# The prices of tensor engine instructions in the planner of a two-layer streaming encoder step

## The chip, the core and the metric

The kernel runs as one launch on one core of a Trainium2 chip. The metric is device time in microseconds, from runs of the whole program. The core has a tensor engine (PE in the profile, its weight loads PEld), a vector engine (DVE), a scalar engine (ACT), GpSimd (POOL) and SyncE (SP), which issues most of the transfers. Each engine takes its own instructions strictly in the order in which the program lists them and waits on semaphores for what other engines make.

## The reference, cut to what matters

One inference step of a two-layer encoder for 384 tokens of width 1024: a sample group of 8 streams with 16 tokens each, and a prompt of 256 tokens. The two groups share all weights.

```
for each layer i:
    x += 0.5 * post(SwiGLU_1(pre(x)))        # 1024 -> 2816 -> 1024
    x +=       post(Mixer_i(pre(x)))         # layer 0: convolution module, layer 1: gated DeltaNet
    x +=       post(MemXAttn(pre(x), mem))   # 4 heads, 256 memory tokens per stream
    x += 0.5 * post(SwiGLU_2(pre(x)))
# pre, post: RMSNorm with gains.  The prompt's memory keys and values: mem @ xa_wk, mem @ xa_wv
```

Everything is float32. Beside the two streams of tokens the step returns the prompt's memory keys and values, the last rows of the convolutions and the recurrent states.

## The kernel before, in words

**Tiling.** Tokens lie in three tiles of 128: the sample group, then two of the prompt. Features lie in tiles of 128 as well. The eight sublayers are called f00, conv, x0, f01, f10, dn, x1 and f11 here, for feed-forward, convolution, cross-attention and DeltaNet of layers 0 and 1.

**Products.** A float32 weight chunk of 128 x 1024 is loaded (`raw`), rounded by ACT to a part `whi` and completed by DVE to a part `wlo` (method `get`). The activations are split likewise (`hTh`, `hTl`, or `rbh`, `rbl`). A product is then three matmuls in the type F32R. Projections (`gmm`) have 384 moving columns, one matmul for all tokens; down and output projections (`dmm`) and some first projections (`wide`) have 512. Small products (attention scores, DeltaNet's matrices, the prompt's memory keys and values) are plain float32 matmuls, each of which shows as two records in the profile. The sample group's attention uses `quad`: four products with 32 stationary columns each, which the tensor engine holds side by side; one `quad` shows as eight records. Transposes are matmuls with the identity (`tr`).

**Two stages make the order.** First, class `Emitter` records all operations with a price each, `cost`, in nanoseconds. It carries a running clock of the tensor engine, `vt`, which `mm`, `quad` and `tr` advance by their price. Work beside the main stream (the norms between sublayers in `chain`, attention heads, DeltaNet heads) is written as generators; `pump` and `until` let such a task take its next step once `vt` has reached the time that the task named. So `vt` sets in which order operations are recorded, and with it which PSUM bank and which columns of the shared tile `big` each of them gets.

Second, class `Scheduler` (method `order`) takes the recorded operations with their dependences and makes a list schedule on modelled engines. Each operation has a `path`, the longest way of prices and hand-over times (`LAT`) to the end of the program. Whenever a modelled engine comes free, it takes, of the operations that are ready by then, the one with the largest `path` plus `bonus` (the constants CHB, HALF and RUSH). The order so found is the order of the instructions in every engine's queue, the transfers of SP among them. Dependences between the operations of one PSUM bank are kept by the whole bank, so four `quad`s into one bank are a chain.

**Between sublayers.** `tokenwise` finishes a sublayer token tile by token tile and starts `chain` for each: a square sum on ACT, a root on POOL (`rstd`: an addition and a power), DVE products, a second root, DVE products, eight transposes, and the split. Pieces of the prompt's memory keys and values (`kv`, 32 pieces of 16 float32 matmuls each) depend on little; the main stream offers a number of them at several places, to be used where the tensor engine would stand still. In cross-attention, `head` makes for every head the scores (four `quad`s into one bank, four products of 256 columns into another), softmax, transposes, the products with the values (again four and four), transposes.

Of the kernel before, what the change touches and what calls it, by code (L numbers as in the profile page):

```python
# [17 lines left out]
KT = 8                  # feature tiles of d_model  # L18
NTOK = 384              # columns: 128 of the sample group (8 streams x 16), then 256 of the prompt
TT = 3                  # token tiles: sample, prompt 0, prompt 1  # L20
FF = 22                 # feature tiles of d_ff
NB = 8                  # sample streams
BL = 16                 # tokens of one
NH = 8                  # DeltaNet heads
XH = 4                  # cross-attention heads
MEM = 256
CW = 31
SW = 4
EPS = 1e-6
W = 8                   # split weight chunks on chip  # L30
RAW = 3                 # raw chunks on chip
# order of the first transfers: memory (m), key and value chunks (c), rows (x), identity, gains
START = ["c0a", "m0a", "c0b", "m0b", "m1", "i", "x1", "g", "c1", "x2", "x0", "c2"]
TOLD = CW - BL          # taps that reach no token of the same step
OLD = 10                 # feature tile of the first sublayer from which these are worked on
CHB = 4000.0            # ns by which what belongs to a token tile goes before the same of the next
RUSH = 10000.0          # ns by which a sublayer's last projections go before the rest
NRUSH = 3               # feature tiles that this holds for
SLOTS = 4               # chunks of keys and values on chip at the start
FOUR = ["f01", "f10", "f11", "x0", "x1"]     # sublayers whose first 512 features are made token tile by token tile  # L40
# first projections of a sublayer that begin before the last token tile is there
SPLIT = {"f00": 0, "conv": 0, "x0": 1, "f01": 0, "f10": 0, "dn": 1, "x1": 2, "f11": 0}
# pieces of the memory's keys and values that a place in the program offers the tensor engine
KV = {"start": 3, "f00": 3, "conv": 20, "co": 3, "xo": 0, "f01": 1, "f10": 2, "dn": 6, "f11": 0}
HALF = 1400.0            # ns by which the first half of a row goes before the second
GROUPS = [(0, 1), (2, 3, 4, 5, 6, 7)]   # heads whose decays are made together
TAIL = 3                # down-projection chunks that go token tile by token tile
LANES = 8               # transfers under way on a queue
DMA_IN, DMA_OUT = 650.0, 950.0
HOP = 100.0             # ns from an engine to the next  # L50
BIG = 17300             # words of the shared region

# columns of the per-feature table
# [5 lines left out]
# constant matrices: causal blocks, block sums, decay masks, block-doubling masks  # L59
# [34 lines left out]
class Emitter:  # L94
    """Records the program in issue order. Tasks beside the main stream are advanced by running
    clocks of the engines, so that their matmuls fall where their operands are ready."""
# [141 lines left out]
    def mm(self, out, lhsT, rhs, start, stop, skip=False):  # L238
        n = self._n(rhs)
        if rhs.dtype == F32R:  # L240
            cost = max(107.0, n / 2.4) + 3
        else:
            cost = 2 * max(107.0, n / 1.2) + 2
        self.vt += cost
        t = self.nc.tensor
        kw = {"skip_group_check": True} if skip else {}
        self._add("P", cost, lambda: t.matmul(out, lhsT, rhs, start=start, stop=stop, **kw), [lhsT, rhs], [out])  # L247
        return self.vt + HOP

    def quad(self, mms):  # L250
        """Products into four groups of 32 rows, which the tensor engine works on at once."""
        n = self._n(mms[0][2])
        cost = 2 * max(107.0, n / 1.2) + 85.0
        self.vt += cost
        t = self.nc.tensor

        def go():
            for out, lhsT, rhs, start, stop in mms:
                t.matmul(out, lhsT, rhs, start=start, stop=stop)  # L259
        self._add("P", cost, go, [x for m in mms for x in m[1:3]], [m[0] for m in mms])  # L260
        return self.vt + HOP

# [13 lines left out]
    def get(self, name, dest=None):  # L276
        """The two parts of a weight chunk: loaded and split as early as their room is free."""
        j = self.nchunk
        self.nchunk += 1
        raw = self.raw[j % RAW]  # L280
# [23 lines left out]
class Scheduler:  # L304
    """Orders the recorded program: a list schedule by the longest way to the end, on the engines'
    known costs, that keeps every dependence between the operations."""
# [8 lines left out]
    def cell(self, ap):  # L315
        """(what, bits): the tile and the columns in it that an operand covers."""
# [32 lines left out]
    def graph(self):  # L349
        ops = self.ops  # L350
        readers, writers = {}, {}
        for i, o in enumerate(ops):
# [3 lines left out]
            for what, bits in rs:  # L356
                if what is not None:
                    pred.update(j for b, j in writers.get(what, ()) if b & bits)
                    if what[0:2] == "ps":
                        # two engines don't read a bank at once  # L360
# [79 lines left out]
class Region:  # L440
    """First-fit allocation of the columns of one tile."""
# [5 lines left out]
    def take(self, n, keep=0, high=False):  # L447
# [13 lines left out]
        # of the places at an edge of a hole, the one whose columns were freed the longest ago  # L461
# [19 lines left out]
class Model:  # L481
# [42 lines left out]
    def alloc(self, n, keep=0):  # L524
        """(columns, handle) for the main stream."""
# [19 lines left out]
    def _bank(self):  # L545
# [3 lines left out]
        # the one that has been free for longest  # L549
# [38 lines left out]
    def rows(self, kind, i):  # L588
        """A row of gains on all partitions."""
# [4 lines left out]
    def rstd(self, s1, s2, dep):  # L594
        """(s1 + s2) ** -0.5."""
# [6 lines left out]
    def chain(self, t, y, yb, gpost, gpre, half=False, cross=False):  # L602
        """x += post(y); the next sublayer's normalized input, transposed and split."""
# [8 lines left out]
        if y is not None:  # L612
            ss, s0 = self.st(2), self.st(1)
            f = 4.0 if half else 1.0    # half of the norm: a root of four times the mean square
            for n in range(2):
                # the two banks, one to an engine at a time
# [15 lines left out]
        for n in range(2):  # L632
# [3 lines left out]
            # behind the row stands what its sum of squares is short of  # L636
# [21 lines left out]
    def gmm(self, out, hi, lo, c0=0, c1=NTOK, h=None, l=None):  # L658
        """out[feature, token] of a chunk [k, 8, 128 features] and the transposed activations."""
# [12 lines left out]
    def dmm(self, y, hi, lo, ah, al, first, last, halves=(0, 1)):  # L672
        """y[token, 1024] += activations [k, 128 tokens] times a chunk of rows."""
# [9 lines left out]
    def first_chunks(self, names, chains, split):  # L683
        """The first projections of a sublayer; some of them on two token tiles before the third is there."""
# [18 lines left out]
    def wide(self, o, w, t):  # L703
        """out[token, 512] of a token tile and four pieces of weights [k, 2, 512]."""
# [14 lines left out]
    def turn(self, a, o, e):  # L719
        """Four blocks of columns, transposed."""  # L720
# [11 lines left out]
    def gains(self, post, pre):  # L732
        """Rows of gains: of the norm behind a sublayer and of the next one's."""
# [98 lines left out]
    def tokenwise(self, acc, held, ops, ready, first, gpost, gpre, ghs, before=None, kv=0, late=False, half=False):  # L832
        """The last chunks of a product into the residual, token tile by token tile, each followed by
        its norms in the background."""
# [30 lines left out]
    def kv_open(self, slots=2, order=()):  # L865
        """Room for pieces of the memory's keys and values: the memory, some weight chunks, two results."""
# [14 lines left out]
    def early(self, what, order):  # L881
        """The first transfers of all go in a given order."""
        self.E.bonus = 1e9 - 1e6 * order.index(what) if what in order else 0.0

    def kv_part(self, out, name, what, order):
        """One of the first transfers in two halves, so that the products can begin with the first."""
# [16 lines left out]
    def kv(self, n):  # L903
        """Some pieces of the memory's keys and values. They wait for nothing else and go where the
        tensor engine would stand still."""
# [40 lines left out]
    def old_taps(self):  # L946
        """The taps that reach only tokens of earlier steps for all of a step's tokens."""
# [17 lines left out]
    def conv(self, chains, post, pre):  # L965
# [4 lines left out]
        HW = CW - TOLD + BL - 1     # tokens of a block and those before it that the later taps reach  # L970
# [27 lines left out]
        def taps():  # L998
            for c0 in range(0, KT, 2):
# [5 lines left out]
                for j in range(CW):  # L1005
                    for c in cs:
# [4 lines left out]
                        elif j < TOLD:  # L1011
                            # the prompt's tokens that have a token that far behind
# [236 lines left out]
    def deltanet(self, chains, post, pre):  # L1249
# [40 lines left out]
        def pre_task(o, b, e):  # L1290
            """Gates of all heads and the decays between all tokens."""
# [39 lines left out]
            for hs in GROUPS:  # L1331
# [12 lines left out]
                # one behind the other, so that the scalar engine changes its table once  # L1344
# [5 lines left out]
        def short(o, b, e, ti):  # L1350
            """Short convolution and SiLU of one feature tile; (columns, handle, ready)."""
# [17 lines left out]
        def head(h, q, k, v):  # L1369
# [51 lines left out]
            def unit(t):  # L1421
                """Decayed products of keys and queries, and the inverse's transpose by block doubling."""
# [6 lines left out]
                # blocks of up to 32 tokens lie one below the other in 32 columns: the transposes of the  # L1429
                # inverse so far and of what it makes of the matrix, which one product brings on together  # L1430
# [21 lines left out]
                if t:  # L1452
                    # pairs of blocks of 32 tokens, then the two of 64
# [35 lines left out]
            # sample: the state's part of the keys and queries, even and odd streams apart  # L1489
# [4 lines left out]
            # prompt, first chunk: no state yet  # L1494
# [61 lines left out]
            # output norm and gate  # L1556
# [107 lines left out]
def consts():  # L1664
    """Constant matrices that depend on shapes alone."""
# [13 lines left out]
def pack(inp):  # L1679
    """The inputs in the order in which the program reads them: layout alone."""  # L1680
# [3 lines left out]
    def g_type(a, c0, n=P):  # L1684
        # [1024, n] -> [p, k, n]
# [8 lines left out]
    for n, i in CHUNK.items():  # L1694
# [5 lines left out]
        elif t in ("g4", "u4", "q4"):  # L1700
            # [1024, 512] -> [p, 2 k, 512]
# [29 lines left out]
    # [l, b, m, h, (c p)] -> [l, h, u, p, b, c, m]  # L1731
# [58 lines left out]
```

## Time and profile before

| What | Value |
|---|---|
| Time of three runs | 1892.46, 1894.15, 1896.69 us; median 1894.15 us |
| Span of the profiled execution | 1891.9 us, 27912 instructions |
| Median of the runs less that span | 2.25 us |
| PE busy | 1870.6 us, 99% of the span |
| PEld busy | 1682.6 us, 89% |
| DVE, ACT, POOL busy | 1025.5, 794.5, 168.8 us |
| Mean traffic | 146 GB/s to and from HBM |

The span runs from the first to the last instruction of one profiled execution; the page gives no other time of that execution, and what lies around the span is taken as the 2.25 us to the median. The stages can be told by the rows of the trace: f00 to about 297 us, conv to 515, x0 to 640, f01 and f10 to 1182, dn to 1480, x1 to 1608, f11 to the end. Matmuls overlap, so that a record's mean duration is longer than the time from its start to the next one's start; the latter is what one matmul costs in a row of them.

### The profile page before, as it was taken

How to read it: one execution, taken by the hardware profiler on the slowest of the kernel's cores; microseconds unless marked ns; L12 is line 12 of the kernel's file. 1: busy time of each engine (PE TensorE's matmuls, PEld its weight loads, DVE VectorE, ACT ScalarE, POOL GpSimd, SP SyncE). 2: the span in 40 equal slices, each digit the busy share in tenths (PEclk: the TensorE clock that was granted, in tenths of full speed). 3: DMA queues.
4: the chain of work that ended last, by engine and by line, in shares of the span. 5: the costliest groups of instructions: out<-in, count | busy, mean ns of one | idle time of the engine just before them, and what ended most of it. 6: DMA issues, size and time to landing. Idle time of an engine off the chain costs nothing.

```text
span 1891.9 us, 27912 instructions
## 1 busy us (share of the span) xinstructions
PE 1870.6 (99%) x10863; PEld 1682.6 (89%) x10863; DVE 1025.5 (54%) x1940; ACT 794.5 (42%) x1589; POOL 168.8 (9%) x407
## 2 busy tenths in 40 slices
PE   8999999999999999999999999999999999999998
PEld 7999999999877899999899999989898767899997
DVE  6564436998653633334633344788886734533333
ACT  4333334312643533233433233787786533433332
POOL 1000002111100100000100000323321101000000
PEclk9999999999999999999999999999999999999999
DMA  8544434556685443434533343433324782444431
GB/s 300 179 136 125 134 112 121 128 147 216 219 312 210 156 129 128 134 123 130 163 122 117 120 134 101 128 97 99 123 90 124 236 311 101 134 134 134 122 123 45
DMA packets 88469, 278.83 MB, mean 147 GB/s; under 512 B 18001, under 2 KB 20561, under 8 KB 88337
## 3 DMA queue, kind: packets, MB, share of 16 engines
q1 hardware_dynamic: 86080, 271.42, 44.7%
q0 software_dynamic: 2256, 5.64, 0.9%
q8 instruction: 85, 1.39, 0.3%
q14 instruction: 48, 0.39, 0.1%
HBM read 265.09 MB, written 11.92 MB: 146 GB/s over the span
## 4 chain that ended last, share of the span: by engine, by line
PE 97%; ACT 1%; DMA 1%; DVE 0%; POOL 0%; issue 0%; SPq 0%; DVEq 0%; POOLq 0%; ACTq 0%
PE ps L247 91%; PE ps L266 3%; PE ps L259 2%; DMA raw<-in_w 0%; POOL stat L197 0%; ACT big L190 0%; DMA x<-in_x 0%; DVE big L210 0%; ACT whi L189 0%; SPq L270 0%; ACT big L189 0%; ACT hTl L190 0%; ACT L190 0%; DVE big L197 0%; DVE wlo L197 0%
## 5 line engine op out<-in xcount | busy, mean ns | idle before, releaser
L197 DVE TENSOR_TENSOR wlo<-raw,whi 128x1024 fp32r<-128x1024 f32 x361 | 438.1, 1221 | 570.7 <-ACT whi L189 542.7
L189 ACT CAST whi<-raw 128x1024 fp32r<-128x1024 f32 x361 | 374.5, 1050 | 640.3 <-PE ps L247 584.6
L247 PE MATMUL ps<-hTh,wlo 128*128 128x384 f32 x1680 | 498.3, 341 | 0.0
L247 PE MATMUL ps<-hTl,whi 128*128 128x384 f32 x1680 | 497.1, 342 | 0.0
L247 PE MATMUL ps<-hTh,whi 128*128 128x384 f32 (+1 forms) x1680 | 496.9, 342 | 0.0
L247 PEld LDWEIGHTS ps<-hTl,whi 128*128 128x128 f32 x1680 | 308.9, 188 | 8.0 <-issue 2.1
L247 PEld LDWEIGHTS ps<-hTh,whi 128*128 128x128 f32 x1680 | 308.8, 188 | 7.9 <-issue 1.2
L247 PE MATMUL ps<-big 128*128 128x128 f32 (+5 forms) x1944 | 308.0, 288 | 7.1 <-DMA big<-in_w 6.7
L247 PEld LDWEIGHTS ps<-hTh,wlo 128*128 128x128 f32 x1680 | 308.7, 188 | 6.5 <-issue 2.3
L247 PEld LDWEIGHTS ps<-big 128*128 128x128 f32 (+1 forms) x1944 | 269.6, 190 | 40.3 <-issue 20.8
L247 PE MATMUL ps<-whi,rbh 128*128 128x512 f32 x672 | 206.0, 396 | 0.4 <-ACT big L189 0.4
L247 PE MATMUL ps<-wlo,rbh 128*128 128x512 f32 x672 | 203.8, 395 | 0.0
L247 PE MATMUL ps<-whi,rbl 128*128 128x512 f32 x672 | 202.5, 393 | 0.0
L210 DVE SCALAR_TENSOR_TENSOR big<-big,cols 128x384 f32<-128x384 f32 (+13 forms) x424 | 189.5, 497 | 2.2 <-ACT big L190 0.3
L247 PEld LDWEIGHTS ps<-whi,rbl 128*128 128x128 f32 x672 | 125.7, 188 | 24.7 <-issue 0.4
L247 PEld LDWEIGHTS ps<-wlo,rbh 128*128 128x128 f32 x672 | 125.3, 188 | 24.6 <-issue 0.4
L247 PEld LDWEIGHTS ps<-whi,rbh 128*128 128x128 f32 x672 | 124.8, 188 | 21.1 <-ACT big L189 0.6
L197 DVE TENSOR_TENSOR big<-big,ps 128x64 f32<-128x64 f32 (+4 forms) x219 | 86.4, 405 | 39.8 <-PE ps L247 39.2
L266 PE MATMUL ps<-ident,big 128*128 128x128 f32 x479 | 89.5, 279 | 5.5 <-DVE big L210 5.4
L247 PE MATMUL ps<-whi,hTh 128*128 128x512 f32 x240 | 87.2, 399 | 0.7 <-ACT hTh L189 0.7
L189 ACT COPY big<-ps 32x32 f32<-32x32 f32 (+5 forms) x155 | 49.6, 324 | 90.2 <-PE ps L247 64.3
L247 PE MATMUL ps<-whi,hTl 128*128 128x512 f32 x240 | 86.3, 398 | 0.0
(82 smaller groups left out, 1350.7 us busy)
## 6 DMA issues: line engine op xcount, KB each, us to landing
raw<-in_w SPq DMA_DIRECT2D x362, 512.0 KB, 3.8
big<-in_w SPq DMA_DIRECT2D x37, 512.0 KB, 5.1
big<-in_ck SPq DMA_DIRECT2D x32, 512.0 KB, 6.5
big<-in_cv SPq DMA_DIRECT2D x32, 512.0 KB, 6.3
big<-in_npre SPq DMA_DIRECT2D x8, 512.0 KB, 7.5
out_pkv<-big POOLq DMA_DIRECT2D x32, 128.0 KB, 5.0
big<-in_npost SPq DMA_DIRECT2D x8, 512.0 KB, 7.3
big<-out_pkv SPq DMA_DIRECT2D x8, 512.0 KB, 5.1
```

Source lines behind the costliest of these rows:

```text
L189: return self._on("A", cost, dep, lambda: sc.copy(out, in_), [in_], w)
L197: return self._on(eng, cost, dep, lambda: e.tensor_tensor(out=out, in0=a, in1=b, op=op), [a, b], [out])
L210: lambda: v.scalar_tensor_tensor(out=out, in0=a, scalar=s, in1=b, op0=op0, op1=op1), [a, s, b], [out])
L247: self._add("P", cost, lambda: t.matmul(out, lhsT, rhs, start=start, stop=stop, **kw), [lhsT, rhs], [out])
L259: t.matmul(out, lhsT, rhs, start=start, stop=stop)
L266: self._add("P", 109.0, lambda: t.transpose(out, in_, ident), [in_, ident], [out])
```

## The change

The prices of tensor engine instructions in `mm` and `quad` get other formulas; n is the number of moving columns. Comments and docstrings of the file are taken out at the same time, which leaves the code and its line numbers as they were.

```
     def mm(self, out, lhsT, rhs, start, stop, skip=False):
         n = self._n(rhs)
         if rhs.dtype == F32R:
-            cost = max(107.0, n / 2.4) + 3
+            cost = max(27.0, (n + 32) / 2.4)
         else:
-            cost = 2 * max(107.0, n / 1.2) + 2
+            cost = 2 * (max(107.0, n / 1.2) + 3)
         self.vt += cost
...
     def quad(self, mms):
         n = self._n(mms[0][2])
-        cost = 2 * max(107.0, n / 1.2) + 85.0
+        cost = 2 * max(107.0, n / 1.2) + 175.0
         self.vt += cost
```

The price of a transpose (109), the prices of the other engines, the hand-over times, the bonuses and all sizes stay. The matmuls, transposes, vector and scalar operations and transfers of the program are the same ones in the same number; what can differ is their order in each queue and the banks and columns that they use.

More of the change, by code (lines that the diff above doesn't have):

```diff
@@ L240, in mm @@
         if rhs.dtype == F32R:
-            cost = max(107.0, n / 2.4) + 3
+            cost = max(27.0, (n + 32) / 2.4)
         else:
-            cost = 2 * max(107.0, n / 1.2) + 2
+            cost = 2 * (max(107.0, n / 1.2) + 3)
         self.vt += cost
@@ L252, in quad @@
         n = self._n(mms[0][2])
-        cost = 2 * max(107.0, n / 1.2) + 85.0
+        cost = 2 * max(107.0, n / 1.2) + 175.0
         self.vt += cost
```

## The prediction

> **What bounds the kernel now.** I read the page first, then the waits of the tensor engine, then start-to-start times in the timeline. The page says that the tensor engine sets the time:
>
> ```profile
> span 1891.9 us, 27912 instructions
> PE 1870.6 (99%) x10863; PEld 1682.6 (89%) x10863; DVE 1025.5 (54%) x1940; ACT 794.5 (42%) x1589; POOL 168.8 (9%) x407
> ...
> PE 97%; ACT 1%; DMA 1%; DVE 0%; POOL 0%; issue 0%; SPq 0%; DVEq 0%; POOLq 0%; ACTq 0%
> ```
>
> PE is busy for all but 21 us of the span, and 97% of the chain of waits is PE's own work. The waits of PE, for the first 24.5 us and for the rest, say where it stands still:
>
> ```profile
> PE ps L247 <- DMA big<-in_w: 6.7, 3, 4.8
> PE ps L266 <- DVE big L210: 1.3, 1, 1.3
> ...
> PE ps L266 <- DVE big L210: 4.1, 3, 3.1
> PE ps L247 <- DVE big L197: 0.9, 1, 0.9
> PE ps L247 <- ACT hTh L189: 0.7, 1, 0.7
> PE ps L247 <- ACT big L189: 0.6, 2, 0.4
> ```
>
> The first two rows are the start: 8.0 us until the first weights and rows have landed. The other four are everything after it: 6.3 us in seven waits, the longest of them 3.1 us. The rest of PE's 21 us is the end of the last token tile, behind the last matmul (a stretch's row has its bounds and length, then busy us and count of PE, PEld, DVE, ACT and POOL, then PE's granted clock, the transfers' share and GB/s):
>
> ```profile
> 1885.00:1892.00 7.00, 0.28 (x2) 0.00 (x0) 3.17 (x5) 0.69 (x2) 0.76 (x2) 0.76 0.40 150
> ```
>
> So a better order has 6.3 us of standing still to win, and what it can save by grouping matmuls more cheaply; a worse order has no such floor.
>
> **The prices against the trace.** A stretch of 384-column matmuls, and the first and last of nine with 512 columns in a row:
>
> ```profile
> 1011.48 0.33 PE L247 MATMUL ps<-hTh,wlo 128*128 128x384 f32 x1
> ...
> 1012.17 1.08 PE L247 MATMUL ps<-whi,rbh 128*128 128x512 f32 x4
> ...
> 1600.11 0.39 PE L247 MATMUL ps<-whi,rbh 128*128 128x512 f32 x1
> ...
> 1601.92 0.39 PE L247 MATMUL ps<-whi,rbl 128*128 128x512 f32 x1
> ```
>
> Four intervals from 1011.48 to 1012.17 are 172.5 ns each. The planner had 384/2.4 + 3 = 163.0 and gets (384 + 32)/2.4 = 173.3. Eight intervals from 1600.11 to 1601.92 are 226 ns each; the planner had 216.3 and gets 226.7. So the new prices hold here, and the old ones were 10.3 ns short. The counts:
>
> ```profile
> L247 PE MATMUL ps<-hTh,wlo 128*128 128x384 f32 x1664 | 494.6, 342 | 0.0
> ...
> L247 PE MATMUL ps<-whi,rbh 128*128 128x512 f32 x672 | 206.0, 396 | 0.4 <-ACT big L189 0.4
> ...
> L247 PE MATMUL ps<-whi,hTh 128*128 128x512 f32 x240 | 87.2, 399 | 0.7 <-ACT hTh L189 0.7
> ```
>
> Each stands for three groups of one size (hi by hi, hi by lo, lo by hi): 4992 matmuls of 384 columns and 3 x (672 + 240) = 2736 of 512, by 10.3 ns: the planner's tensor clock runs 80 us longer, about 4% of the span. The float32 price rises by 4 ns (216 to 220 at 128 columns), the quad's from 511.7 to 601.7. No matmul is added or removed, so the work itself is **0**; all that follows is order.
>
> [...]
>
> **Part 1, quads among other matmuls.** In `xattn` a head's four quads fill one bank and four products of 256 columns another, with the same softmax steps behind both, so the planner picks by how much of each chain is left. Old: quads 4 x 511.7 = 2047, products 4 x 428.7 = 1715. It takes a quad (1535 left), then a product since 1715 is more (1286 left), and so on: Q M Q M Q M Q M, four runs of quads. The trace shows this form, and elsewhere a run of four:
>
> ```profile
> 594.58 0.64 PE L259 MATMUL ps<-big 128*32 128x256 f32 x8
> 595.15 0.70 PE L247 MATMUL ps<-big 128*128 128x256 f32 x2
> 595.78 0.64 PE L259 MATMUL ps<-big 128*32 128x256 f32 x8
> 596.35 0.70 PE L247 MATMUL ps<-big 128*128 128x256 f32 x2
> ...
> 541.43 1.93 PE L259 MATMUL ps<-big 128*32 128x256 f32 x32
> 543.29 1.13 PE L247 MATMUL ps<-big 128*128 128x256 f32 x4
> ...
> 546.12 1.56 PE L247 MATMUL ps<-big 128*128 128x256 f32 x6
> 547.61 0.64 PE L259 MATMUL ps<-big 128*32 128x256 f32 x8
> ```
>
> New: 4 x 601.7 = 2407 against 4 x 432.7 = 1731. A quad leaves 1805, still more than 1731, so a second follows (1203 left), then two products, then they alternate: Q Q M M Q M Q M, three runs. A lone quad takes 0.57 us to the next start and a lone product 0.63. Four quads in a row take 1.86 us, so each further one 0.43; three products in a row take 1.49 us, so each further one 0.43. Q Q M M is 0.57 + 0.43 + 0.43 + 0.63 = 2.06 us against 2.40 for Q M Q M: **0.34 us for each run saved**. There are 16 groups (4 heads, 2 layers, scores and values). Other heads' matmuls and projections fall between them and break the form, as in the second stretch; I take 6 of the 16: **-2.0 us**, with 0 and 16 x 0.34 = -5.4 as the bounds.
>
> **Part 2, the standing still.** With tensor prices that were 6% short, the planner believed the tensor engine to be earlier than it is. What it placed just in time behind ACT, DVE or POOL therefore came with some room on the chip: PE needs longer for the matmuls in between, and the operand is there. Right prices take this room away, and what shows then is how well the other prices hold. The norms between sublayers go over POOL twice:
>
> ```profile
> L197 POOL TENSOR_TENSOR stat<-stat,negh 128x1 f32<-128x1 f32 x51 | 34.9, 684 | 7.0 <-DVE stat L204 3.2
> ...
> L197 POOL TENSOR_TENSOR stat<-stat 128x1 f32<-128x1 f32 x48 | 18.4, 383 | 101.7 <-ACT big L190 56.8 <-ACT hTl L190 44.5
> ```
>
> The planner has 465 and 132 ns for these (`tt` with eng="G"); the rows have 684 and 383, though POOL's spans are rough. Two of each per token tile make 2 x (219 + 251) = 0.94 us by which a `chain` is longer than planned. The four transposes behind it are what the row of waits "PE ps L266 <- DVE big L210" names. Behind such a transpose every later matmul is queued, since PE keeps its order. Bounds: the seven waits vanish, -6.3 us; or one wait of 0.94 us comes at each of the seven boundaries between the eight sublayers, +6.6 us. The 3.1 us one is a boundary (x1 to f11, by when all pieces of `kv` are used up), so a price alone does not fill it. I take **+1.0 us**, near the middle.
>
> **Part 3, the rest of the order.** `vt` hands out banks and columns in another order, and SP's queue follows. Bounds: one more or one less wait as long as the longest now, 3.1 us either way; I take **0**. The load of weights is far ahead of use in most of the program, so SP's new order is covered there; in the two attention stages it is not (second rival below). The start hangs on transfers whose order is fixed by START, and the end on one token tile's norm: **0**.
>
> **Sum.** 0 - 2.0 + 1.0 + 0 + 0 = -1.0 us: span 1890.9 us, and with the 2.25 us around it a median of 1893.15, so **1893 us**. About 0.2%, 3.8 us, is what a measurement of this kernel can tell from no change, so this counts as no change.
>
> **The rivals.**
>
> Slower, by the chains. If Part 2 goes to its upper end, with Part 1 at 0, the time is 1894.15 + 6.6 = 1901 us. For it: the prices of POOL are short by the rows above, and a wait of this very kind is already the longest. Against it: now only three such waits exist after the start, and where filling matmuls are left the planner may put more ahead. It decides where the matmuls queued ahead of the transposes are fewer than the chain is late, and shows as more waits of L266 on L210.
>
> Slower, by the keys and values. In the attention stages transfers are near their most:
>
> ```profile
> 520.30:567.60 47.30, 47.19 (x356) 33.64 (x355) 24.11 (x43) 20.00 (x46) 1.17 (x3) 1.00 0.89 312
> 1513.60:1560.90 47.30, 47.30 (x363) 32.66 (x362) 17.80 (x37) 17.81 (x48) 0.00 (x0) 1.00 0.87 311
> ```
>
> If the columns for one head's keys come free later, its eight loads of 0.5 MB land later; at 312 GB/s those 4.2 MB are 13 us, half of which other matmuls should cover: +7 us a layer, 1901 in one layer. Against it: PE waits for none of these loads in either slice now.
>
> Faster. Part 1 at all 16 groups (-5.4) and half of the body's waits gone (-3.1): 1885.6 us. For it: the plan now has the right clock for 97% of the chain. Against it: the longest wait has nothing to fill it.
>
> The planner's order hardly differs: if few comparisons of `path` turn, the time stays at 1894. It falls into "no change".
>
> [...] As a mechanism of this kernel: were the whole span packed like the slice below, where weight loads fill 44.45 of 47.30 us (94%), it would take 1682.6/0.94 = 1790 us.
>
> ```profile
> 993.30:1040.60 47.30, 47.30 (x252) 44.45 (x251) 17.67 (x19) 14.34 (x19) 0.00 (x0) 1.00 0.37 116
> ```
>
> The attention slices above, with 33 of 47 us, are full of matmuls too and wait for nothing; their loads are smaller. I give it 1 in 100.
>
> **How the numbers follow.** My forecast, with the case that little differs: 0.46. Slower by the chains 0.17, by the keys and values 0.10, together 0.27. Faster 0.26, and 0.01 for the packed span, together 0.27. The forecast's own range is 1890.4 to 1897.9. For 8 in 10 I reach to the faster case and to both slower ones with a little over: 1886 to 1903.
>
> **What would show it.** Part 1: of the rows of L259 in the attention stages, fewer of x8 and more of x16; L259's place in the timeline shows 0.43 us for a second quad. Part 2: the waits of PE after 24.5 us, by name; over 10 us in sum is the first rival. The second rival shows as waits of L247 or L259 on in_ck or in_cv. Unchanged steady stretches (172.5 and 226 ns) would show that the work is the same. I am wrong if the time leaves 1890.4 to 1897.9, and wrong in kind if it does so without the waits or the quads moving.

## The result and the profile after

The changed kernel takes 1920.5 us (median of four runs, 1916.84 to 1921.32) against 1893.77 us for the kernel before in the same comparison (1892.46 to 1896.69). The ratio is 1.0137 with an interval of 1.0122 to 1.0153: slower by 1.4%, well outside the range forecast.

The page of the changed kernel, its span, its busy times and the shares of the chain that ended last:

```profile
span 1918.3 us, 27924 instructions
...
PE 1885.6 (98%) x10863; PEld 1686.8 (88%) x10863; DVE 1020.7 (53%) x1940; ACT 791.3 (41%) x1587; POOL 173.0 (9%) x407
...
PE 66%; DVE 5%; ACT 3%; DMA 2%; POOL 1%; issue 1%; POOLq 0%; DVEq 0%; SPq 0%; ACTq 0%
```

PE has the same 10863 matmul records and is still busy for 98% of the span. But the chain of waits, which was 97% PE before, now leaves PE for DVE, ACT and transfers in many places: many operands arrive at the moment when they are needed or later. The span grew by 26.4 us. PE's time without work grew from 21.3 us (1891.9 - 1870.6) to 32.7 us (1918.3 - 1885.6), that is by 11.4; PE's busy time grew by 15.0 us for the same work.

The waits of PE in the changed kernel after 24.5 us (us in total, times, longest):

```profile
PE ps L266 <- DVE big L210: 6.4, 6, 3.3
PE ps L247 <- ACT big L190: 3.1, 6, 0.9
PE ps L247 <- DVE hTl L197: 2.0, 4, 0.9
PE ps L247 <- POOL stat L197: 1.4, 2, 0.7
PE ps L247 <- DVE big L210: 1.1, 1, 1.1
PE ps L266 <- ACT hTh L189: 0.6, 1, 0.6
PE ps L266 <- DVE big L197: 0.6, 1, 0.6
PE ps L247 <- ACT hTh L189: 0.5, 1, 0.5
PE ps L247 <- ACT big L189: 0.5, 1, 0.5
PE ps L247 <- DVE big L197: 0.2, 1, 0.2
```

These are all of them: 16.4 us in 24 waits, against 6.3 us in seven before. By name, the transposes behind the norms (the first row) have 2.3 us of these 10.1; it was 4.1 us in three. But what stands between two sublayers waits under other names too, its splits and first matmuls. By place, the boundaries between sublayers have 8.6 us against 4.7, DeltaNet's heads 3.9 against 0.2, the convolution 2.5 against 0.9, the start of f00 behind 24.5 us has 1.0 against none, and the rest 0.5 against 0.4. None is on a transfer of keys or values.

A steady stretch of the changed kernel, from the timeline (start, us of one record, instruction):

```profile
1009.17 0.33 PE L247 MATMUL ps<-hTh,wlo 128*128 128x384 f32 x1
1009.34 0.33 PE L247 MATMUL ps<-hTl,whi 128*128 128x384 f32 x1
1009.51 0.33 PE L247 MATMUL ps<-hTh,wlo 128*128 128x384 f32 x1
```

The matmuls follow one another by 0.17 us as before. So a steady stretch costs what it did, and the 26 us come with the order. A record of 0.33 us reaches past the next one's start, so a delay of up to 0.16 us shows as busy time and not as a wait.

**Where they are.** A stage is bounded here by its first 384-column matmul. The boundaries inside conv and x0 and inside dn and x1 move with the order, so each pair is taken together. First the kernel before, conv with x0 and dn with x1 (bounds and length, busy us and count of PE, PEld, DVE, ACT, POOL, PE's granted clock, the transfers' share, GB/s):

```profile
312.60:658.50 345.90, 344.48 (x2253) 300.40 (x2252) 241.82 (x430) 134.28 (x255) 46.85 (x80) 1.00 0.61 195
1195.90:1642.40 446.50, 441.38 (x2798) 373.14 (x2798) 303.96 (x883) 285.39 (x793) 87.53 (x240) 1.00 0.44 147
```

The same stages of the changed kernel:

```profile
313.80:667.10 353.30, 348.78 (x2266) 301.76 (x2266) 241.14 (x430) 131.52 (x252) 45.20 (x77) 1.00 0.60 191
1208.60:1668.70 460.10, 449.58 (x2785) 376.42 (x2784) 301.57 (x881) 280.30 (x789) 88.83 (x243) 0.98 0.42 139
```

| Stages | Longer by | of it PE without work | of it PE busy |
|---|---|---|---|
| dn and x1 | 13.6 us | 5.4 | 8.2 |
| conv and x0 | 7.4 us | 3.1 | 4.3 |
| the rest (differences to the whole) | 5.4 us | 2.9 | 2.5 |
| whole span | 26.4 us | 11.4 | 15.0 |

The windows do not hold quite the same work. In conv and x0 the changed kernel has 13 records more, 12 of them of float32 products with 128 columns, which follow one another by about 0.114 us (65 in a row took 7.42 us in the kernel before): by this estimate 1.4 of the 4.3 us. In dn and x1 it has 13 fewer, 12 of them short split products that now stand ahead of the stage's first 384-column matmul, so that slightly more than 13.6 us is lost there.

**Why PE is busy longer in dn and x1.** The granted clock there is 0.98 on average, and it is lost in three places. Windows of the changed kernel, first the 3.4 us ahead of each place, then the places themselves (columns as above):

```profile
1346.20:1349.60 3.40, 2.11 (x14) 1.60 (x14) 2.97 (x14) 3.35 (x13) 1.65 (x7) 1.00 0.54 157
...
1510.10:1513.50 3.40, 1.40 (x7) 0.75 (x7) 3.40 (x7) 3.40 (x10) 0.57 (x1) 1.00 0.55 154
...
1626.10:1629.50 3.40, 1.19 (x6) 0.65 (x4) 2.93 (x4) 3.40 (x12) 1.71 (x2) 1.00 0.01 2
```

```profile
1513.50:1516.90 3.40, 3.40 (x7) 2.47 (x8) 2.90 (x4) 1.13 (x3) 1.76 (x2) 0.50 0.00 0
...
1629.50:1636.30 6.80, 5.75 (x20) 5.07 (x21) 6.56 (x10) 5.39 (x11) 2.74 (x7) 0.50 0.26 77
...
1349.60:1356.40 6.80, 6.62 (x25) 5.82 (x26) 3.69 (x14) 5.59 (x23) 0.61 (x3) 0.50 0.01 4
```

In order of time, PE worked for 2.11, 1.40 and 1.19 of 3.4 us, and then ran at half clock for 6.8, 3.4 and 6.8 us. That is 17.0 us at half clock, against 3.4 us in the kernel before (granted 0.50 from 1605.27 to 1608.68 us, beside its one long wait). If all work in these stretches took twice its time, half of the difference, **6.8 us**, is lost to the clock, of the 8.2 us by which PE is busy longer in dn and x1. This is an upper bound: of the four runs of the change, those with a mean clock of 0.994 and 0.995 took 1921.0 and 1920.0 us, those with 0.997 took 1921.3 and 1916.8.

The second place is the boundary from dn to x1 and the third that from x1 to f11, as was the one of before. So of the 17.0 us, 10.2 stand behind norms and 6.8 among DeltaNet's heads.

The first place is inside the DeltaNet heads. Its timeline in the changed kernel (in brackets the idle time before a record and what ended it):

```profile
1343.42 0.33 PE L247 MATMUL ps<-hTh,wlo 128*128 128x384 f32 x1
...
1347.36 1.91 PE L247 MATMUL ps<-big 64*64 64x64 f32 x12 [0.88 <-ACT big L190]
1349.78 2.83 PE L247 MATMUL ps<-big 128*128 128x128 f32 x10 [0.50 <-ACT big L190]
...
1353.75 0.67 PE L247 MATMUL ps<-hTh,whi 128*128 128x384 f32 x1
```

Between 1343.42 and 1353.75 us no projection stands in PE's queue, only the heads' small products and transposes. The two waits among them, 0.88 and 0.50 us, are for what ACT made of earlier ones.

### The profile page after: what moved, and what is told of

It is laid out like the page before. It is cut to its first block, busy times and chain, and to the rows that moved or that the text cites. A ratio compares the mean times of both kernels' runs of the same rounds, so it can differ in the third digit from the quotient of the medians.

```text
span 1918.3 us, 27924 instructions
## 1 busy us (share of the span) xinstructions
PE 1885.6 (98%) x10863; PEld 1686.8 (88%) x10863; DVE 1020.7 (53%) x1940; ACT 791.3 (41%) x1587; POOL 173.0 (9%) x407
## 4 chain that ended last, share of the span: by engine, by line
PE 66%; DVE 5%; ACT 3%; DMA 2%; POOL 1%; issue 1%; POOLq 0%; DVEq 0%; SPq 0%; ACTq 0%
PE ps L247 62%; DVE big L210 3%; PE ps L266 2%; PE ps L259 2%; DMA raw<-in_w 2%; ACT big L190 2%; POOL stat L197 1%; ACT whi L189 1%; DVE wlo L197 1%; DVE big L197 1%; DMA big<-in_alog 0%; ACT big L189 0%; POOL big L215 0%; ACT hTl L190 0%; DVE x L210 0%
## 5 line engine op out<-in xcount | busy, mean ns | idle before, releaser
L247 PE MATMUL ps<-hTh,whi 128*128 128x384 f32 x1680 | 493.5, 343 | 2.4 <-ACT big L190 1.7
L247 PE MATMUL ps<-hTl,whi 128*128 128x384 f32 x1680 | 491.6, 342 | 0.5 <-DVE hTl L197 0.5
L247 PE MATMUL ps<-hTh,wlo 128*128 128x384 f32 x1680 | 491.6, 341 | 0.0
L247 PE MATMUL ps<-big 128*128 128x128 f32 (+5 forms) x1944 | 311.4, 291 | 10.6 <-DMA big<-in_w 6.9
L247 PEld LDWEIGHTS ps<-hTh,whi 128*128 128x128 f32 x1680 | 308.4, 188 | 14.7 <-ACT big L190 3.9
L247 PEld LDWEIGHTS ps<-hTl,whi 128*128 128x128 f32 x1680 | 308.8, 188 | 9.2 <-issue 2.1
L247 PEld LDWEIGHTS ps<-hTh,wlo 128*128 128x128 f32 x1680 | 308.0, 188 | 5.6 <-issue 1.8
L247 PEld LDWEIGHTS ps<-big 128*128 128x128 f32 (+1 forms) x1944 | 271.5, 191 | 45.2 <-issue 14.1
L247 PE MATMUL ps<-whi,rbh 128*128 128x512 f32 x672 | 206.3, 396 | 0.0
L247 PE MATMUL ps<-wlo,rbh 128*128 128x512 f32 x672 | 206.3, 395 | 0.0
L247 PE MATMUL ps<-whi,rbl 128*128 128x512 f32 x672 | 202.2, 395 | 0.0
L210 DVE SCALAR_TENSOR_TENSOR big<-big,cols 128x384 f32<-128x384 f32 (+11 forms) x424 | 187.2, 507 | 3.0 <-ACT big L190 1.6
L247 PEld LDWEIGHTS ps<-wlo,rbh 128*128 128x128 f32 x672 | 125.6, 188 | 25.2 <-issue 1.5
L247 PEld LDWEIGHTS ps<-whi,rbl 128*128 128x128 f32 x672 | 125.3, 188 | 24.0 <-issue 0.4
L247 PEld LDWEIGHTS ps<-whi,rbh 128*128 128x128 f32 x672 | 125.1, 188 | 22.2 <-issue 1.1
L197 DVE TENSOR_TENSOR big<-big,ps 128x384 f32<-128x384 f32 (+4 forms) x219 | 87.0, 407 | 70.9 <-PE ps L247 51.8
L266 PE MATMUL ps<-ident,big 128*128 128x128 f32 x479 | 90.2, 280 | 9.4 <-DVE big L210 7.8
L247 PE MATMUL ps<-whi,hTl 128*128 128x512 f32 x240 | 86.4, 405 | 1.6 <-DVE hTl L197 1.6
L247 PE MATMUL ps<-whi,hTh 128*128 128x512 f32 x240 | 86.9, 405 | 0.2
L204 POOL TENSOR_SCALAR stat<-stat 128x1 f32<-128x1 f32 (+2 forms) x48 | 13.7, 286 | 801.9 <-ACT hTl L190 785.9
```

What stands on the lines that cost most here:

```text
L197: return self._on(eng, cost, dep, lambda: e.tensor_tensor(out=out, in0=a, in1=b, op=op), [a, b], [out])
L204: return self._on(eng, cost, dep, lambda: e.tensor_scalar(out=out, in0=a, scalar1=s1, scalar2=s2, op0=op0, **kw), [a, s1, s2 if s2 is not ...
L210: lambda: v.scalar_tensor_tensor(out=out, in0=a, scalar=s, in1=b, op0=op0, op1=op1), [a, s, b], [out])
L266: self._add("P", 109.0, lambda: t.transpose(out, in_, ident), [in_, ident], [out])
```

## The experiments

All ratios are against the kernel before on the same chip; 0.1% is 1.9 us.

**Which price.** One price family at a time.

```
e1_f32r:     if F32R: cost = max(27.0, (n + 32) / 2.4)            # the rest as before
e2_quad_f32: float32: cost = 2 * (max(107.0, n / 1.2) + 3); quad: ... + 175.0
```

> Only the F32R price is changed (384 columns 163.0 to 173.3 ns, 512 columns 216.3 to 226.7); float32 and quad prices stay as before. Theory 'room' (short tensor prices let every operand of ACT, DVE and POOL arrive early; right prices take this away): nearly all of the +26.7 us, so 1913 to 1921 us, PE's waits after the first 24.5 us at 15 us or more. Theory 'scatter' (any change of a price draws another order, and the one before is a good draw): anything from 1890 to 1925, not bound to the size of the change. Theory 'quads' (the quad price of 601.7 turns the attention order): below 1900.

> Only the quad price (511.7 to 601.7 ns at 256 columns) and the float32 price (216 to 220 at 128 columns) are changed; F32R prices stay. These are 11 us of the 91 us that the planner's tensor clock gains. 'Room': at most an eighth of the loss, 1892 to 1897 us. 'Scatter': it may move by 5 to 25 us although hardly any price moved. 'Quads': 1910 to 1921 us.

The F32R price alone: 1915.38 against 1892.53 us, ratio 1.0126 (1.0109 to 1.0143). The other two: 1.0036 (1.0023 to 1.0049). Nearly all comes with the price of the split products, the one by which the planner's tensor clock gained its 80 us. But the two parts add up to 31 us, and the second, at 1900 us, lies outside the 1892 to 1897 that lost room was to give.

**Which stage of the planner.** The new prices only in the recorder's clock, or only in the list schedule.

```
e3_clock_new:  self.vt += new;  cost = old      # in mm and quad
e4_plan_new:   self.vt += old;  cost = new
```

> The new prices advance the recorder's clock vt alone; the planner's own price of each operation stays as before. If the loss comes from the recording (when tasks step, which bank and which columns they get): 1913 to 1921 us. If it comes from the list schedule ('room'): 1892 to 1898 us. 'Scatter': neither this one nor its mirror needs to be near 1894, and the two losses need not add up to 26.7 us.

> The mirror: the planner prices each operation anew, the recorder's clock keeps the old prices. 'Room' in the list schedule: 1912 to 1921 us, with PE's waits after 24.5 us at 15 us or more. From the recording: 1892 to 1898 us. 'Scatter': no sum rule with its mirror.

The recorder's clock alone: 1.0063 (1.0048 to 1.0078), 12 us. The list schedule alone: 1.0084 (1.0067 to 1.0101), 16 us. Together 28, about the whole. So neither stage has the whole loss, as the expectations would have had it for one or the other, and the paths that Part 1 rests on are not all of it: the order in which heads and projections are recorded costs 12 us by itself.

**Is it the right price, or any other price?** The kernel before with its F32R price moved by a constant.

```
-            cost = max(107.0, n / 2.4) + 3
+            cost = max(107.0, n / 2.4) - 7        # f2_minus_ten
+            cost = max(107.0, n / 2.4) + 2.5      # i2_minus_half
+            cost = max(107.0, n / 2.4) + 3.5      # f1_plus_half
+            cost = max(107.0, n / 2.4) + 8.15     # i1_plus_five
+            cost = max(107.0, n / 2.4) + 23.6     # f4_plus_twenty
```

> The kernel before with F32R prices 0.5 ns longer (163.0 to 163.5 at 384 columns), a twentieth of the change. 'Room': a twentieth of the loss, 1892 to 1895 us. 'Good draw' (the constants of the kernel before fit its own order, and any other order is worse by chance): 1896 to 1908 us.

> The kernel before with F32R prices 10 ns shorter (163.0 to 153.0 at 384 columns): as far from before as the change, the other way, and further from the trace. 'Room': every operand has still more room, PE's waits after 24.5 us stay near 6 us or fall, 1885 to 1897 us. 'Good draw': 1903 to 1920 us, as with the change. 'Accuracy' (a plan is the better the nearer its prices are to the chip): slower as well, 1905 to 1925.

> The kernel before with F32R prices 20.6 ns longer (163.0 to 183.6 at 384 columns), twice the step of the change; the tensor engine is now too slow in the plan by 6%. 'Room': the loss about doubles, 1930 to 1945 us, with PE's waits after 24.5 us at 30 us or more. 'Good draw': 1905 to 1922 us, no more than the change. 'Accuracy': above the change's 1915, as the prices are wrong again.

> The kernel before with F32R prices 5.15 ns longer, half of the change. A loss that grows with the price lies between +4 and +24: 1902 to 1910 us, DeltaNet at 313 to 318 us. If any other order costs the same: 1895 to 1901 us or, as a step, 1912 to 1918.

> The kernel before with F32R prices 0.5 ns shorter. The chance of a new order alone, with no room taken: 1893 to 1900 us, as with +0.5 ns (1897), -10 ns (1899) and the 300 ns (1893). Above 1903 us, chance alone would be as large as half of the loss.

| F32R price against before | Ratio | Interval | us |
|---|---|---|---|
| -10 ns | 1.0032 | 1.0020 to 1.0044 | +6 |
| -0.5 ns | 1.0016 | 1.0006 to 1.0026 | +3 |
| +0.5 ns | 1.0021 | 1.0011 to 1.0030 | +4 |
| +5.15 ns | 1.0050 | 1.0034 to 1.0066 | +9.5 |
| +10.3 ns (e1; 24 matmuls of 128 columns got cheaper) | 1.0126 | 1.0109 to 1.0143 | +24 |
| +20.6 ns | 1.0204 | 1.0189 to 1.0220 | +39 |

Two things are in this table. A change of half a nanosecond either way tells the planner next to nothing about the chip, and yet costs 3 to 4 us: the order before is a good draw among its neighbours, and the orders beside it lose a little. On top of that comes a trend, about 2 us for each ns by which the tensor engine is priced higher. A price 10 ns lower, twice as far from the trace as the one before, loses only 6 us. So being nearer to the trace gained nothing, and a higher price cost more than a lower one. There is one run on the far lower side, which lay between what lost room and what a good draw were to give, and at +20.6 ns PE's waits were 20.4 us where 30 had been expected of lost room.

**Is it the lost room?** If higher tensor prices harm because the other engines' prices are too low beside them, then raising those should undo it.

```
f3_others_up (on the change):  HOP 100 -> 106; every cost but PE's and every LAT x 1.06
g1_room_after (on the change), g2_room_before (on the kernel before), in order():
+                if s.eng == "P" and e in "AVG":
+                    s.ready = max(s.ready, end + self.LAT[e].get("P", 150) + 300.0)
g3_pool (on the change): POOL's tt 132 -> 380, its power 300 + 165 n -> 520 + 144 n
g4_fast_clock (on the change): in order(), PE's clock takes F32R at cost - 10.3
```

> The changed kernel with the prices of ACT, DVE and POOL, all hand-over times and HOP 6% longer, so that the tensor engine is again short against them by what it was before. 'Room': it comes back, 1890 to 1900 us, PE's waits after 24.5 us at 10 us or less. 'Good draw': it stays at 1905 to 1920 us, since the order is a new one.

> The changed kernel, whose list schedule takes an operand that ACT, DVE or POOL makes to be at the tensor engine 300 ns later than the hand-over time says (only for the time when a matmul counts as ready, not for the paths). If the loss is that operands come too late for the queue's order ('room', as a length of time): 1895 to 1906 us and PE's waits after 24.5 us back from 17 us to 8 us or less. If the loss lies elsewhere in the order: above 1910 us, with the waits down all the same or not.

> The same 300 ns in the kernel before. 'Room': the seven waits of 6.3 us shrink, 1887 to 1893 us. 'Good draw': another order, 1896 to 1905 us, as with the half nanosecond (1897) and the ten shorter (1899).

> The changed kernel with POOL's prices set to the trace as well (an addition or product 132 to 380 ns, a power of one column 465 to 664). The prediction's rival 'by the chains': each norm was planned 0.94 us short, which shows once the tensor prices are right; then this takes back 5 us or more, to 1900 to 1913 us, and the waits of L266 on L210 fall from 6.4 us to 4 us or less. If the chains' prices are not it: 1914 to 1923 us.

> The changed kernel, whose list schedule lets the tensor engine's clock run at the old F32R prices, while the paths (which of the ready operations goes first) and the recorder's clock keep the new ones. If the schedule's clock is the place of the loss: near the run with the new prices in the recorder's clock alone, 1900 to 1907 us. If the paths are it: 1915 to 1921 us.

All others up by 6%: 1.0093 (1.0077 to 1.0110). Room of 300 ns ahead of PE: 1.0098 (1.0083 to 1.0113) on the change, and 1.0002 (0.9992 to 1.0012), nothing, on the kernel before. The schedule's own clock at the old price: 1.0111 (1.0096 to 1.0126), about 5 us back, with intervals that meet. POOL's prices from the trace: 1.0119 (1.0104 to 1.0134), not told apart from the change itself. Its waits of PE after 24.5 us:

```profile
PE ps L266 <- DVE big L210: 4.8, 4, 2.8
```

The transposes' waits went from 6.4 to 4.8 us, but other waits grew, to 19.3 us in sum.

The two runs that give room back return 7 to 8 us of 26, but not by the mechanism: I had expected PE's waits after 24.5 us at 10 and 8 us or less, and they were 15.9 and 15.2, against 16.4 in the change. Both times also lie in the ranges that the expectations gave to a loss of another kind. So lost room is not shown as a cause; that another order by itself loses 7 to 8 us less fits as well. And correcting POOL's prices, the ground of my first rival, brought nothing that can be told from none.

**Where.** The new prices inside the DeltaNet sublayer only, or everywhere but there.

```
+        E.dn = True
         ch = self.deltanet(ch, 5, 6)
+        E.dn = False
h1_dn_alone:    cost = new if self.dn else old
h2_all_but_dn:  cost = old if self.dn else new
```

> New tensor prices for what is recorded inside the DeltaNet sublayer, old ones everywhere else. 'DeltaNet' (the loss sits in this stage, where the heads' small products and the projections that cover them share eight banks): 1903 to 1909 us, the stage near 322 us instead of 310. 'All over': 1893 to 1899 us.

> The reverse: old prices inside the DeltaNet sublayer, new ones everywhere else. 'DeltaNet': 1902 to 1909 us, the stage back to 309 to 314 us, the other 13 us being in the start, the convolution and the attentions. 'All over': 1912 to 1919 us.

DeltaNet alone: 1.0063 (1.0046 to 1.0080), 12 us. All but DeltaNet: 1.0077 (1.0062 to 1.0092), 15 us. The sum is again the whole. The window of dn and x1 with the new prices in DeltaNet alone:

```profile
1195.60:1655.70 460.10, 447.46 (x2799) 376.30 (x2799) 302.50 (x883) 280.41 (x791) 89.01 (x243) 0.99 0.42 141
```

And with them everywhere but there:

```profile
1208.60:1656.70 448.10, 442.04 (x2785) 371.73 (x2785) 297.33 (x880) 277.47 (x789) 90.71 (x243) 1.00 0.43 144
```

460.1 us is what the full change has, and 448.1 is close to the 446.5 of before. What dn and x1 lose, they lose by the prices inside DeltaNet.

**By what, there.** On the full change, either the recorder's clock `vt` alone takes the old prices inside DeltaNet, or three of the eight PSUM banks are kept for the projections in DeltaNet's loop over heads.

```
h4_dn_clock_old:  self.vt += old if self.dn else cost
h3_three_banks:   self.own = (0, 1, 2)                    # around the loop over heads
                  free = [b for b in range(8) if self.bank_free[b] and (main or b not in self.own)]
```

> The changed kernel; only inside DeltaNet does the recorder's clock run at the old prices (the planner's prices stay new everywhere). If the jumps come from when the heads' steps are recorded: 1906 to 1914 us, the stage at 310 to 317 us. If the planner's prices make them: 1915 to 1921 us.

> The changed kernel; in DeltaNet's loop three of the eight PSUM banks are kept for the projections, the heads share the other five (the projections may take any). 'Banks' (projections are ready but their bank is still held by a head whose work ACT and DVE have not finished): 1905 to 1913 us, the stage at 310 to 317 us, the 16 to 17 us jumps between the starts of successive projections gone. 'Clock in DeltaNet, not banks': 1914 to 1922 us.

The clock: 1.0084 (1.0069 to 1.0099), 10 us back of the change's 26. Its window of dn and x1, with 10.8 us less than the change:

```profile
1208.80:1658.10 449.30, 440.64 (x2785) 370.05 (x2784) 297.25 (x881) 272.12 (x785) 91.09 (x243) 1.00 0.43 144
```

The banks: 1.0080 (1.0065 to 1.0095), and 8.6 us less in the window:

```profile
1206.60:1658.10 451.50, 445.51 (x2804) 372.23 (x2803) 304.42 (x883) 283.52 (x793) 88.73 (x243) 1.00 0.43 144
```

In the first of the two, the list schedule still has every new price. Taken by itself, that says that inside DeltaNet the harm is done when the program is recorded, before anything is scheduled. The runs of one stage at a time do not agree. Their windows of dn and x1, first with the new prices in the recorder's clock alone, then in the list schedule alone:

```profile
1198.10:1650.00 451.90, 443.94 (x2800) 373.76 (x2799) 302.68 (x883) 281.18 (x791) 90.31 (x243) 1.00 0.43 143
```

```profile
1203.80:1662.40 458.60, 449.43 (x2806) 376.40 (x2805) 304.71 (x883) 286.64 (x793) 89.88 (x240) 0.99 0.43 143
```

That is 5.4 and 12.1 us more than before. In the second the recorder's clock has the old prices in DeltaNet too, and the stage loses nearly all that it loses in the change. (Its profiled execution took 6.3 us more than its median, that of the first 3.4 less; with these taken off and put on, 5.8 and 8.8 us remain.) So the old clock inside DeltaNet mends this one order, and which stage does the harm is not separated.

The waits of the run with the old clock in DeltaNet are telling in another way; the largest rows after 24.5 us (an added line shifts the line numbers by one):

```profile
PE ps L267 <- DVE big L211: 3.4, 7, 1.3
PE ps L248 <- ACT big L191: 2.9, 4, 1.5
PE ps L248 <- DVE hTl L198: 2.5, 5, 0.9
PE ps L248 <- ACT hTh L190: 2.2, 3, 1.1
```

All nine rows add up to 15.7 us, hardly less than the 16.4 of the change. But none is longer than 1.5 us, and the granted clock is 0.999 over the span, against 0.995 in the change. Of the 10.8 us in the window, 8.9 are PE's busy time (449.58 to 440.64), about what 17.0 us at half clock would cost at most, 8.5; 1.9 are time without work.

Some of this is chance. At the boundary from dn to x1 both kernels have the same waits by name (L266 or L267 on L210 1.7 us in two, L247 or L248 on hTl 0.9 us). The two windows of 3.4 us around them in the run with the old clock:

```profile
1502.30:1505.70 3.40, 1.98 (x13) 1.41 (x13) 3.40 (x7) 2.90 (x9) 1.62 (x4) 1.00 0.66 181
1505.70:1509.10 3.40, 2.26 (x10) 1.49 (x11) 3.40 (x6) 3.14 (x8) 0.00 (x0) 1.00 0.75 289
```

Here they are shared out between two windows, and both ran at a granted clock of 1.00. In the change PE worked for 2.72 us of one and 1.40 of the next, and 3.4 us at 0.50 followed, up to 1.7 of the 10.8 us. Curing the half clock without changing the order was not tried.

Of all these, none beats the kernel before; the one with room on top of it equals it.

## Why the prediction was wrong

**The work, 0.** Right, as far as the steady stretches show, which are unchanged; the number of matmuls is the same.

**Part 1, quads, -2.0 us.** Right in sign, too large. From the timeline of the changed kernel, a head whose four quads and four products are both ready:

```profile
604.34 0.70 PE L247 MATMUL ps<-big 128*128 128x256 f32 x2
604.97 0.64 PE L259 MATMUL ps<-big 128*32 128x256 f32 x8
605.53 0.70 PE L247 MATMUL ps<-big 128*128 128x256 f32 x2
```

Quads still alternate with products here. The runs of quads in the two attention stages fell from 46 to 43, which at 0.34 us each is -1.0 us.

**Part 2, standing still, +1.0 us with +6.6 as the upper bound.** The direction was right, the size was not, and the place was half of it. PE waits 10 us more. The boundaries between sublayers, on which I had put all of it, have 3.9 us of that, and up to 3.4 us more by the half clock behind them (10.2 us of it against 3.4). As much again, 3.6 us of waits and up to 3.4 by the clock, comes from DeltaNet's heads, which I had taken to be covered as before.

**Part 3, the rest of the order, 0 with 3.1 us either way. This is the step that failed.** I wrote that `vt` hands out banks and columns in another order, with SP's queue behind it, and bounded all that by one wait as long as the longest. No row stood for that bound, and I had said myself that a worse order has no floor. Of the 26.4 us by which the span grew, the quads have -1.0 and the waits at the boundaries 3.9; about 23 us are left for this term and for the clock. The new prices cost 12 us in the recorder's clock alone and 16 in the list schedule alone. By place, DeltaNet's prices alone make all of the 13.6 us of dn and x1: heads stand there without projections among them, PE waits (0.88 and 0.50 us), and its granted clock is 0.50 from 1349.6 to 1356.4 us. `vt` decides when a task beside the main stream takes its next step, and so how many projections are recorded between two steps of a head; that keeping banks for the projections gives back 8.6 us there fits the reading that projections could not be issued while the heads held the banks. The same banks were not tried on the kernel before, and the list schedule alone loses nearly as much in this stage, so this is support and not proof. The failed step is known, the mechanism behind it only in part.

**A term that was missing.** The bounds of Parts 2 and 3 took a wait to cost its length. Some cost more: 17.0 us at a granted clock of 0.50 follow them, against 3.4 us before, up to 6.8 us in all. Of the other 8.2 us by which PE is busy longer, delays too short to show as waits may be a part. Outside the half clock, those intervals from one 384-column matmul to the next that exceed 178 ns have 29.8 us beyond 173 ns each, against 26.5 before: 3.3 us. For the rest no cause is shown.

**The first rival, slower by the chains, 1901.** Its sign came: waits over 10 us, and six of L266 on L210 where there were three. With the half clock the boundaries may even have lost its 6.6 us, a quarter of the whole. But the ground that I gave for it, POOL's prices, did not bear it out: correcting them gave no gain that could be told from none. **The second, keys and values,** fell: no such wait. **The faster case** fell as well. Its ground was that the plan now had the right clock for most of the chain; the table of prices shows that being nearer to the trace in this price is worth nothing here. That the planner's other prices, hand-over times and constants had been settled together with the old one would explain it, but no run shows this: raising the others by 6% gave back 8 us of 26.

**What stays open.** For the 12.8 us outside dn and x1 the place is known, not the cause. They hold no half clock ahead of the last matmul (granted 1.00 there in every stretch of 48 us). In conv and x0 PE lost 3.1 us without work and 4.3 us by longer busy time, of which some 1.4 us are work from elsewhere. The trend of 2 us per ns is measured; that it goes through DeltaNet's prices is shown for 12 us of the change, by which stage of the planner is not.

## What to carry to other kernels

Treat a planner's prices as part of its tuning and not only as a description of the chip: a price that was right by the trace made this order 24 us worse, and no wrong one that was tried made it better. Before trusting a corrected price, time a few wrong ones around it, half a unit as well as twice as far; if half a nanosecond costs 4 us, then that is a first measure of the scatter of orders, and only what clearly exceeds it can belong to the price. When an experiment on a part seems to name the cause, hold it against the runs that changed one stage alone. Where a tensor engine is near 99% busy, a bound for a worse order has to count the clock granted behind a sparse stretch, not only the waits: here 17.0 us at 0.50, up to 6.8 us lost, beside 16.4 us of waits.

## What the runs showed of the hardware

I had not expected the clock to matter in a kernel that is 99% busy. In the changed kernel's timeline behind the longest wait, at the boundary from x1 to f11:

```profile
1630.55 2.82 PE L266 MATMUL ps<-ident,big 128*128 128x128 f32 x12 [3.26 <-DVE big L210]
...
1634.02 0.63 PE L247 MATMUL ps<-whi,hTl 128*128 128x512 f32 x1
1634.45 0.63 PE L247 MATMUL ps<-whi,hTh 128*128 128x512 f32 x1
...
1637.18 0.39 PE L247 MATMUL ps<-whi,hTl 128*128 128x512 f32 x1
1637.41 0.39 PE L247 MATMUL ps<-whi,hTh 128*128 128x512 f32 x1
```

A matmul of 512 columns takes 0.43 us to the next start, and 3 us later 0.23 us again. Ahead of the last matmul, the stretches at half clock (granted 0.50) are 3.4 or 6.8 us long in these two kernels. The three of the change start 163.9 and 116.0 us apart, which is 48 and 34 times the 3.41 us that the stretch of before lasts (1605.27 to 1608.68). A wait of 3.1 us before was followed by 3.4 us of half clock, one of 3.3 us after by 6.8 us. At 1346 us no such wait came first: the longest gap with nothing but small products around it was 0.88 us. In the three windows above, which end where the half clock begins, PE was busy for 62, 41 and 35% of the 3.4 us. In these two kernels that share does not decide alone, for in the kernel before a window with 62%, whose start lies 119.5 us (35 times 3.41 us) ahead of its half clock, was followed by full clock:

```profile
1485.80:1489.20 3.40, 2.10 (x12) 1.14 (x10) 3.13 (x6) 2.81 (x8) 1.77 (x4) 1.00 0.95 281
1489.20:1492.60 3.40, 3.40 (x14) 2.37 (x13) 3.40 (x6) 3.13 (x7) 1.05 (x2) 1.00 0.73 276
```

What decides was not shown.
